# A hybrid encoder layer on one core: the forget gates' row and the first queries issued later, one chunk of values earlier

## The chip, the cores and the metric

The kernel runs on one core of one Trainium2 chip. The metric is the device time of one execution in microseconds; lower is better. The core has five engines that run side by side, each working off its own queue in order: TensorE (PE in the profile; its weight loads are PEld), VectorE (DVE), ScalarE (ACT), GpSimd (POOL), and SyncE (SP), which issues most of the DMA transfers. TensorE writes its results to PSUM, eight banks that VectorE and ScalarE read. Engines wait for each other only through semaphores: an instruction that waits holds up all that stand behind it in its own queue.

## The reference

One layer of a bidirectional encoder on 1024 tokens of width 1024, in float32. Cut to what matters:

```
mod = silu(c) @ w_ada + b_ada                      # six rows: shifts, scales, gates
h = modulate(rms_norm(x), sh1, sc1)
q_a, k_a, v_a, qk_m, v_m, o_m, gates = split(h @ w_in)
y_attn = attention(rope(norm(q_a)), rope(norm(k_a)), v_a)          # 8 heads of 64, 2 key heads
q, k = silu(conv5(qk_m))                                           # a 5-tap convolution along the tokens
i, f = gates (forward and backward); log_f = log_sigmoid(f)
h_fw, h_bw = mlstm(q, k, v_m, i, log_f), the same from the end     # 4 heads of 128
y_mem = norm(h_fw + h_bw) * sigmoid(o_m)
x = x + g1 * (concat(y_attn, y_mem) @ w_out)
x = x + g2 * ((silu(h2 @ w_gate) * (h2 @ w_up)) @ w_down),  h2 = modulate(rms_norm(x), sh2, sc2)
return rms_norm(x)
```

## The kernel before

**Products.** Each float32 product is made of three matmuls in a rounded format (`mm3`, L323 to L325): both operands are split into a high part (ScalarE, a copy: hh, whi) and the rest (VectorE or GpSimd, a subtraction: hl, wlo). Weights arrive by DMA as pieces (wst), are split into whi and wlo, and wait in a ring of six.

**A plan written as a program.** The order of all instructions is fixed before the run. The kernel's source steps through a clock of its own (`Clock`): chains of steps are put on a list of events with planned durations, and as the clock passes, each step issues its instruction. So each engine's queue holds its instructions in the order of planned times. The chip follows that order, but not the planned times: where it is later than planned on one engine, instructions behind the late one wait. `ck.chain(delay, step, step, ...)` starts after `delay` planned us; a Flag among the steps holds the chain until it is set; `LAT` = 0.14 lies between steps. A step that sets `ck.fin` lengthens itself to that time.

**Streams.** TensorE's work comes from generators. Main streams go first when they are ready, and fill streams take the rest (`streams`). The fill stream `un` works off the list `IN`, the units of the input projection:

- ("q", i): a pair of attention heads' queries;
- ("f", i): 128 channels of qk_m. `conv_unit` makes two halves of 512 tokens, 24 matmuls each into one PSUM tile acc; ScalarE evacuates each half to xp, and then VectorE runs five taps on all 1024 tokens (y), ScalarE a tanh, VectorE the last product, and SP stores y;
- ("t", i): 256 columns of v_m or o_m for all tokens, in eight blocks of 24 matmuls into acct; ScalarE evacuates each block to vstg and SP stores it. ("t", 1) is the second half of the values v_m, for the heads 2 and 3 of the memory; it needs four pieces of weights, a convolution unit two.

**The switch to attention.** `IN` first runs alone. When the last queries are rotated and stored (rope_ok[3]), the forget gates' logarithm is issued (logf_ok) and no sum is open in PSUM, the plan stops the stream between two halves or units (`ready`), closes the pool ps0 (six banks for acc and acct, two for the rest, among them ms) and opens ps1: one buffer for acc and acct together, two for T, two double ones for S, one for av. Then it calls `att_q(0)`, sets `attending`, and runs three main streams with `un` as fill: `scores` (S = queries times keys, VectorE's maximum sst, ScalarE's exp P, GpSimd's division), `turned` (transposes of P into T, split to PT by ScalarE and VectorE) and `values` (av). The first split of queries, `att_q(0)`, is a ScalarE copy to qs (high part) and a VectorE subtraction of its lower half; later heads have theirs on GpSimd.

**The gates.** `gate_steps` handles the 16 gate rows in two lists. The first ends with `logf`: VectorE writes the logarithm of the forget gates into T (T1 in the source). The second waits for logf_ok and `attending`; its first step `moved` is ScalarE's copy of that row to Fr. Then follow a mask (GpSimd), four scans, and the ends and rows (VectorE), exponentials (ScalarE), transposes and the last factors. `run(steps, apart, ...)` paces a list: `paced` sets `ck.fin = max(ck.fin, ck.now + apart)` after each step, and the second list has `apart` = PACE = 10.0, so its steps lie at least 10 planned us apart. Its end, gates_ok, is needed after attention only.

At the switch, ScalarE's queue thus has, in this order: the copy to Fr, the copy to qs, and the evacuation of the half that ended at the switch (the first half of ("f", 4)). Most instructions are issued by a helper, L102; they are told apart by their tiles.

Of the kernel before, what the change touches and what calls it, by code (L numbers as in the profile page):

```python
# [14 lines left out]
AF = mybir.ActivationFunctionType  # L15
# [31 lines left out]
AHEAD = 2  # L47
NP = NF // 2
IN = [("q", 2), ("q", 3), ("f", 0), ("f", 4), ("t", 2), ("f", 1),
      ("f", 5), ("f", 2), ("f", 6), ("t", 1), ("f", 3), ("f", 7), ("t", 3)]  # L50
MIX = [("o", i) for i in range(16)] + [("m", (i + 8) % 16) for i in range(16)]
FF = [("b", p) for p in range(NB)] + [("v", 0)] + [("s", (p, i)) for p in range(1, NP - 1) for i in range(2)] + [("v", NP - 1)]
SET = ["A11", "A12", "S2", "S3", "S1", "A22", "S4"]
# [77 lines left out]
class Clock:  # L131
# [12 lines left out]
    def run(self, eng, cost, two=False):  # L144
        s = max(self.free[eng], self.now)
        if two and self.lock and eng in self.two:
            other = "gps" if eng == "dve" else "dve"
            s = max([s] + [b for a, b in self.two[other] if a <= s < b])
            self.two[eng] = self.two[eng][-7:] + [(s, s + cost)]
        e = self.free[eng] = s + cost  # L150
        self.fin = max(self.fin, e)
# [109 lines left out]
def layer_kernel(ctx, tc, xT, c, w_ada, vecs, cons, rope, w_f, w_fT, w_t0, w_t, w_o, w_gu, w_d, out):  # L261
# [65 lines left out]
    def dma(dst, src, q=None):  # L327
        (q or nc.sync).dma_start(dst, src)
        on_chip = dst.space == src.space == bass.MemoryType.SB if hasattr(src, "space") else False
        return ck.dma(math.prod(dst.shape) * 4, 0.65 if on_chip else 0.5)  # L330
# [4 lines left out]
    ck = Clock()  # L335
    dve, act, gps = Engine(ck, nc.vector, "dve"), Engine(ck, nc.scalar, "act"), Engine(ck, nc.gpsimd, "gps")
# [11 lines left out]
    class slot:  # L348
# [11 lines left out]
        t = property(lambda self: self.flag().t)  # L360
# [15 lines left out]
    with tc.manual_schedule():  # L376
# [148 lines left out]
        def row_tile(name, tag="raw"):  # L525
            return gtp.tile([P, S], F32, tag=tag, name=name, bufs={"raw": 3, "row": 1}[tag])
# [434 lines left out]
        gates_ok, logf_ok, attending = Flag(), Flag(), Flag()  # L961
# [34 lines left out]
        def gate_steps():  # L996
# [17 lines left out]
            def soft(i):  # L1014
                if i == 0:
                    G["t"] = stp.tile([P, S], F32, tag="x", name="gt", bufs=KT)[64:P]
                    act.activation(G["t"], G["T1"][64:P], AF.Abs)
                elif i == 1:
                    act.activation(G["t"], G["t"], AF.Exp, scale=-1.0)
                else:  # L1020
                    act.activation(G["t"], G["t"], AF.Ln, bias=1.0)
# [15 lines left out]
            def scan(i):  # L1037
                F, I, mk = G["F"], G["T1"][0:64], G["mk"]
                if i == 0:
                    G["T2"] = row_tile("T2")  # L1040
                    M = G["M"] = G["T2"][0:64]
                    dve.tensor_tensor_scan(M[0:32], F[0:32], I[0:32], 0.0, op0=OP.add, op1=OP.max)
                elif i == 1:
                    dve.tensor_tensor_scan(G["M"][32:64, ::-1], F[32:64, ::-1], I[32:64, ::-1], 0.0,
                                                 op0=OP.add, op1=OP.max)
                elif i == 2:
                    B = G["B"] = F
                    dve.tensor_tensor_scan(B[0:32], mk[0:32], F[0:32], 0.0, op0=OP.mult, op1=OP.add)
                else:
                    dve.tensor_tensor_scan(G["B"][32:64, ::-1], mk[32:64, ::-1], F[32:64, ::-1], 0.0,  # L1050
                                                 op0=OP.mult, op1=OP.add)
# [24 lines left out]
            def exps(i):  # L1076
                if i == 0:
                    each(G["T1"][64:P], G["B"], mprev)
                elif i == 1:
                    act.activation(G["M"], G["M"], AF.Exp, scale=-1.0)  # L1080
                elif i == 2:
                    each(G["T2"][64:P], G["T1"][0:64], rend)
                else:
                    dve.tensor_add(rend, rend, mprev)
                    act.activation(rend, rend, AF.Exp)
# [43 lines left out]
            def run(steps, apart, flag, *before):  # L1129

                def paced(fn):
                    def go():
                        fn()
                        ck.fin = max(ck.fin, ck.now + apart)
                    return go

                out = [(None, f) for f in before]
                for e, f in steps:
                    out.append((e, (f[0], paced(f[1])) if isinstance(f, tuple) else paced(f)))
                ck.chain(0.5, *[f for _, f in out], (lambda: None), bg=[e for e, _ in out] + [None], flag=flag)  # L1140

            run([("gps", spaces), ("dve", spaced), (None, (slot("T"), lambda: rows(0))), (None, (slot("T"), lambda: rows(1))),
                 *[("act", lambda i=i: soft(i)) for i in range(3)], ("dve", logf)], 0.0, logf_ok)
            run([("act", moved), ("gps", mask), *[("dve", lambda i=i: scan(i)) for i in range(4)], ("dve", ends), ("dve", rows_r),
                 ("dve", rows_hl), *[("act", lambda i=i: exps(i)) for i in range(4)],
                 *[(None, (slot("T"), lambda i=i, b=b: columns(i, b))) for i in range(2) for b in range(2)],
                 ("dve", lambda: dve.tensor_scalar(cols[:, :, 1], cols[:, :, 1], QK, None, op0=OP.mult)),
# [24 lines left out]
        Q, Pt, PT = {}, {}, {}  # L1172
# [5 lines left out]
        def att_q(h):  # L1178
            if h:
                qd = ap.tile([P, S], F32, tag="qd", name="qd", bufs=1)  # L1180
                src = q_d[h // 2][(h % 2) * DH:(h % 2 + 1) * DH]
                dma(qd[0:DH], src)
                there = ck.chain(dma(qd[DH:P], src), lambda: None)
            else:
                qd, there = q0_at
            qs = ap.tile([P, S], F32R, tag="qs", name="qs")
            Q[h] = qs, ck.chain(0.0, there, *([] if h else [logf_ok]), lambda: act.activation(qs, qd, AF.Copy),
                                lambda: (gps if h else dve).tensor_sub(qs[DH:P], qd[DH:P], qs[DH:P].bitcast(F32)))

        def scores():  # L1190

            for q in range(NQ):
                h, j = divmod(q, NJ)
                if j == 2 and h + 1 < AH:
                    att_q(h + 1)
                ada_late()
                g, (qs, ok) = h // 4, Q[h]
                yield [ok, k2_ok[g]] + [slot("S")] + Tem[max(q - 3, 0):max(q - 2, 0)]
                sp, f = psum_tile([P, S], "S")
                for n in range(NH):  # L1200
                    for m in range(2):
                        nc.tensor.matmul(sp[:, halves(n)], qs[:, j * P:(j + 1) * P], k2[g][m][:, halves(n)],  # L1202
                                         start=m == 0, stop=m == 1)
                ck.pe(0.87)
                st = ap.tile([P, 4], F32, tag="sst", name="sst", bufs=8)
                cq = colq[:, j, h:h + 1]

                def top(st=st, sp=sp, cq=cq):
                    dve.reduce_max(st[:, 0:1], sp, axis=AX.X)
                    dve.tensor_scalar(st[:, 1:2], st[:, 0:1], cq, -1.0, op0=OP.mult, op1=OP.mult)  # L1210

                def exp(st=st, sp=sp, cq=cq, q=q, f=f):
                    Pt[q] = ap.tile([P, S], F32, tag="P", name="P", bufs=3)
                    act.activation(Pt[q], sp, AF.Exp, bias=st[:, 1:2], scale=cq, accum_out=st[:, 2:3])
                    f.set(ck, ck.fin + LAT)

                def norm(st=st, q=q):
                    gps.tensor_scalar(Pt[q], Pt[q], st[:, 3:4], 0.0, op0=OP.mult, op1=OP.add)

                ck.chain(LAT, top, exp, lambda st=st: dve.reciprocal(st[:, 3:4], st[:, 2:3]), norm, flag=Pok[q])  # L1220
# [968 lines left out]
        for n in range(NH):  # L2189
            def chunk_step(j, k):  # L2190
                ck.need(h_ok[n][k])
                if k == 0:
                    ck.need(slot("acct").flag())
                    tiles.append(psum_tile([P, 272], "acct"))
                s = slice(j * P, (j + 1) * P)
                mm3(tiles[j][0], (h_hi[k][:, s], h_lo[k][:, s]), weights(start["t", 0], k, 2), k == 0, k == KT - 1)
                ck.pe(0.38)
                if k == KT - 1:
                    chunk_out(0, j, *tiles[j])

            js = range(4 * n, 4 * n + 4)
            for k in range(KT - 2):
                for j in js:
                    chunk_step(j, k)
                if k % 2 and (n or k < 4):
                    load_piece()
            for j in js:
                for k in range(KT - 2, KT):
                    chunk_step(j, k)
            if n:  # L2210
                load_piece()
            if n == 0:
                while not again:
                    ck.pop()
                shift_sums()
            else:
                ck.chain(0.0, *vo_ok[0], gate_steps)
# [175 lines left out]
```

## Time and profile before

| | us |
|---|---|
| median of 3 runs | 1325.08 |
| lowest and highest run | 1324.16, 1325.69 |
| the profiled execution | 1330.26 |
| its span, first to last instruction | 1328.5 |
| mean granted TensorE clock | 0.989 |

| engine | busy us | share of the span |
|---|---|---|
| TensorE | 1272.7 | 96% |
| VectorE | 1047.4 | 79% |
| ScalarE | 701.3 | 53% |
| GpSimd | 508.4 | 38% |

The profile records one execution. Times in its rows are us from the first instruction; a row names engine, line, operation, and tiles as out<-in. Idle time before an instruction stands in brackets with the instruction that ended it. Busy shares are means over stages with different limits, so a stage is read by its own rows. The input projection alone runs until 144 us, attention with the units of `IN` beside it until about 481 us; ("t", 2) is the first chunk in it (163 to 233 us), ("t", 1) runs from 346 to 411 us, and ("t", 3) is the last unit.

### The profile page before, as it was taken

How to read it: one execution, taken by the hardware profiler on the slowest of the kernel's cores; microseconds unless marked ns; L12 is line 12 of the kernel's file. 1: busy time of each engine (PE TensorE's matmuls, PEld its weight loads, DVE VectorE, ACT ScalarE, POOL GpSimd, SP SyncE). 2: the span in 40 equal slices, each digit the busy share in tenths (PEclk: the TensorE clock that was granted, in tenths of full speed). 3: DMA queues.
4: the chain of work that ended last, by engine and by line, in shares of the span. 5: the costliest groups of instructions: out<-in, count | busy, mean ns of one | idle time of the engine just before them, and what ended most of it. 6: DMA issues, size and time to landing. Idle time of an engine off the chain costs nothing.

```text
span 1328.5 us, 19724 instructions
## 1 busy us (share of the span) xinstructions
PE 1272.7 (96%) x6656; PEld 1074.3 (81%) x6656; DVE 1047.4 (79%) x1701; ACT 701.3 (53%) x1327; POOL 508.4 (38%) x444
## 2 busy tenths in 40 slices
PE   9999799999999999999999999999999999999997
PEld 7887588788888888787877888888888887788886
DVE  7958798889867865999789988866776755888886
ACT  6583667687767645555586333233323334454453
POOL 0072376676755415432143255555545430000002
PEclk9999899999999999999999999999999999999999
DMA  9557433333323027633552443333333258833325
GB/s 374 186 151 195 130 114 118 102 99 110 119 91 102 25 98 250 217 109 112 188 183 80 141 146 134 107 115 112 103 103 119 72 184 319 311 97 96 95 59 164
DMA packets 104469, 187.04 MB, mean 141 GB/s; under 512 B 11568, under 2 KB 33200, under 8 KB 104368
## 3 DMA queue, kind: packets, MB, share of 16 engines
q1 hardware_dynamic: 91120, 163.81, 38.8%
q10 hardware_dynamic: 13248, 21.97, 4.4%
q8 instruction: 53, 0.87, 0.3%
q14 instruction: 48, 0.39, 0.1%
HBM read 139.33 MB, written 42.73 MB: 137 GB/s over the span
## 4 chain that ended last, share of the span: by engine, by line
PE 64%; DVE 15%; issue 8%; ACT 4%; DMA 4%; POOL 4%; SPq 1%; ACTq 0%; DVEq 0%; POOLq 0%
PE acc L325 17%; PE acc L323 17%; PE acc L324 16%; PE av L1255 2%; PE T L1234 2%; DVE sst L102 2%; DVE y L102 2%; DVE x L102 2%; PE S L1202 2%; DVE PT L102 2%; POOL hl L102 1%; POOL wlo L102 1%; PE acct L323 1%; PE U L1962 1%; PE acct L325 1%
## 5 line engine op out<-in xcount | busy, mean ns | idle before, releaser
L102 ACT ACTIVATE whi<-wst 128x512 fp32r<-128x512 f32 (+2 forms) x223 | 134.0, 606 | 142.1 <-PE acc L325 59.9
L102 POOL TENSOR_TENSOR wlo<-wst,whi 128x512 fp32r<-128x512 f32 x80 | 121.0, 1519 | 177.7 <-ACT whi L102 126.9
L324 PE MATMUL acc<-x,whi 128*128 128x512 f32 x352 | 137.1, 389 | 0.0
L102 DVE TENSOR_TENSOR wlo<-wst,whi 128x512 fp32r<-128x512 f32 (+2 forms) x143 | 94.6, 666 | 34.6 <-ACT whi L102 34.2
L102 POOL TENSOR_SCALAR P<-P,sst 128x1024 f32<-128x1024 f32 x64 | 84.6, 1325 | 76.3 <-DVE sst L102 61.4
L323 PE MATMUL acc<-hh,whi 128*128 128x512 f32 x224 | 97.0, 433 | 9.9 <-ACT xp L102 8.7
L102 POOL TENSOR_TENSOR wlo<-wr,whi 128x512 fp32r<-128x512 f32 x52 | 72.6, 1395 | 72.1 <-ACT whi L102 68.2
L102 DVE TENSOR_TENSOR PT<-T,PT 128x512 fp32r<-128x512 f32 x128 | 84.1, 682 | 20.0 <-ACT PT L102 20.0
L102 POOL TENSOR_TENSOR x<-x,ny 128x256 f32<-128x256 f32 (+1 forms) x8 | 8.3, 1068 | 234.7 <-PE acc L325 214.8
L323 PE MATMUL acc<-whi,wch 128*128 128x512 f32 x244 | 95.7, 392 | 2.5 <-ACT wch L102 2.5
L325 PE MATMUL acc<-whi,wcl 128*128 128x512 f32 x244 | 96.1, 394 | 1.6 <-DVE wcl L102 1.6
L324 PE MATMUL acc<-wlo,wch 128*128 128x512 f32 x244 | 95.6, 392 | 0.0
L102 ACT ACTIVATE PT<-T 128x512 fp32r<-128x512 f32 x128 | 72.9, 596 | 31.6 <-PE T L1234 30.4
L324 PE MATMUL acc<-hl,whi 128*128 128x512 f32 x224 | 88.8, 397 | 0.3 <-DVE hl L102 0.3
L325 PE MATMUL acc<-hh,wlo 128*128 128x512 f32 x224 | 88.9, 397 | 0.1
L102 ACT ACTIVATE P<-S,sst,colq 128x1024 f32<-128x1024 f32 x64 | 77.2, 1206 | 21.5 <-DVE sst L102 20.5
L102 ACT ACTIVATE whi<-wr 128x512 fp32r<-128x512 f32 x56 | 35.4, 632 | 100.5 <-DVE wr L102 48.4
L323 PE MATMUL acct<-whi,hh 128*128 128x256 f32 (+1 forms) x256 | 79.1, 309 | 8.0 <-ACT vstg L102 5.8
L1234 PE MATMUL T<-ident,P 128*128 128x128 f32 x512 | 73.4, 276 | 8.3 <-DVE PT L102 6.5
L102 DVE TENSOR_REDUCE sst<-S 128x1 f32<-128x1024 f32 x64 | 77.7, 1214 | 4.4 <-PE S L1202 3.4
L324 PEld LDWEIGHTS acc<-x,whi 128*128 128x128 f32 x352 | 66.1, 188 | 13.8
L325 PE MATMUL acct<-whi,hl 128*128 128x256 f32 (+1 forms) x256 | 74.1, 289 | 1.9 <-POOL hl L102 1.9
(483 smaller groups left out, 3827.7 us busy)
## 6 DMA issues: line engine op xcount, KB each, us to landing
wr<-in_w_gu_dram SPq DMA_DIRECT2D x66, 256.0 KB, 2.7
ada<-in_w_ada_dram SPq DMA_DIRECT2D x64, 256.0 KB, 3.0
wd<-in_w_d_dram SPq DMA_DIRECT2D x22, 512.0 KB, 6.6
wst<-in_w_gu_dram SPq DMA_DIRECT2D x42, 256.0 KB, 2.9
wst<-act_d SPq DMA_DIRECT2D x33, 256.0 KB, 3.8
ada<-in_w_ada_dram SPq DMA_DIRECT2D x16, 512.0 KB, 7.7
wst<-in_w_o_dram SPq DMA_DIRECT2D x32, 256.0 KB, 3.6
act_d<-sg ACTq DMA_DIRECT2D x29, 256.0 KB, 2.0
```

Of the source, the lines that this page charges most:

```text
L102: return fn(*args, **kw)
L323: nc.tensor.matmul(acc, w[0], x[0], start=first, stop=False)
L324: nc.tensor.matmul(acc, w[0], x[1], start=False, stop=False)
L325: nc.tensor.matmul(acc, w[1], x[0], start=False, stop=last)
L1202: nc.tensor.matmul(sp[:, halves(n)], qs[:, j * P:(j + 1) * P], k2[g][m][:, halves(n)], start=m == 0, stop=m == 1)
L1234: nc.tensor.transpose(tp[:, k], Pt[q][:, (4 * b + k) * P:(4 * b + k + 1) * P], ident)
L1255: nc.tensor.matmul(av, va[:, k, h // 4], PT[it, b][m][:, k - 4 * b], start=(k, m) == (0, 0), stop=(k, m) == (NJ - 1, 1))
L1962: nc.tensor.matmul(U, T[:, i], wv[:, i], start=True, stop=True)
```

## The change

Three edits.

1. The second list of the gates gets a new first step `wait`, which issues nothing and sets `ck.fin` to 6.0 us later. It is paced like the other steps of the list.
2. The chain of `att_q(0)` starts 3.0 planned us after the call instead of at once; the later heads keep 0.0.
3. In `IN`, ("t", 1) moves from behind ("f", 6) to behind ("f", 1), so ahead of ("f", 5), ("f", 2) and ("f", 6).

```diff
 IN = [("q", 2), ("q", 3), ("f", 0), ("f", 4), ("t", 2), ("f", 1),
-      ("f", 5), ("f", 2), ("f", 6), ("t", 1), ("f", 3), ("f", 7), ("t", 3)]
+      ("t", 1), ("f", 5), ("f", 2), ("f", 6), ("f", 3), ("f", 7), ("t", 3)]
...
-            run([("act", moved), ("gps", mask), *[("dve", lambda i=i: scan(i)) for i in range(4)], ("dve", ends), ("dve", rows_r),
+            def wait():
+                ck.fin = ck.now + 6.0
+
+            run([(None, wait), ("act", moved), ("gps", mask), *[("dve", lambda i=i: scan(i)) for i in range(4)], ("dve", ends), ("dve", rows_r),
...
-            Q[h] = qs, ck.chain(0.0, there, *([] if h else [logf_ok]), lambda: act.activation(qs, qd, AF.Copy),
+            Q[h] = qs, ck.chain(0.0 if h else 3.0, there, *([] if h else [logf_ok]), lambda: act.activation(qs, qd, AF.Copy),
                                 lambda: (gps if h else dve).tensor_sub(qs[DH:P], qd[DH:P], qs[DH:P].bitcast(F32)))
```

The instructions are the same in kind and number; what changes is their order in each engine's queue. As the order follows from planned times, the later order can differ in other places too.

## The prediction, made before the changed kernel ran

> **What bounds the kernel now.** I read the page first, then TensorE's waits in the stretch where attention runs (140 to 500 us), then the timelines of TensorE, ScalarE and VectorE around the one large hole, then the clock in short windows.
>
> The page's busy shares, and TensorE's own waits (who waited for whom, total us, times, longest):
>
> ```profile
> PE 1272.7 (96%) x6656; PEld 1074.3 (81%) x6656; DVE 1047.4 (79%) x1701; ACT 701.3 (53%) x1327; POOL 508.4 (38%) x444
> ...
> PE acc L323 <- ACT xp L102: 8.7, 3, 7.0
> ```
>
> TensorE is busy 96% of the span, so over long distances the end moves by what TensorE idles or loses in clock. One wait of 7.0 us stands out: a matmul into acc waits for ScalarE's evacuation of an earlier acc into xp. TensorE's timeline there (start, duration, in brackets the idle time before and its releaser):
>
> ```profile
> 143.64 0.39 PE L325 MATMUL acc<-hh,wlo 128*128 128x512 f32 x1
> 151.01 0.79 PE L323 MATMUL acc<-hh,whi 128*128 128x512 f32 x1 [6.98 <-ACT xp L102]
> ...
> 158.48 1.98 PE L1202 MATMUL S<-k,qs 128*128 128x512 f32 x8
> ...
> 163.27 0.53 PE L323 MATMUL acct<-whi,hh 128*128 128x256 f32 x1 [2.14 <-ACT xp L102]
> ```
>
> At 143.64 + 0.39 = 144.03 the first half of unit ("f", 4) ends. There the plan opens the PSUM pool ps1, and the second half waits until 151.01. ScalarE's queue at that time, complete from 144 to 163 us:
>
> ```profile
> 144.13 0.58 ACT L102 ACTIVATE xp<-acc 128x512 f32<-128x512 f32 x1
> 148.34 1.05 ACT L102 ACTIVATE Fr<-T 64x1024 f32<-64x1024 f32 x1 [3.62 <-DVE T L102]
> 149.41 1.06 ACT L102 ACTIVATE qs<-qd 128x1024 fp32r<-128x1024 f32 x1
> 150.38 0.58 ACT L102 ACTIVATE xp<-acc 128x512 f32<-128x512 f32 x1
> 156.11 0.63 ACT L102 ACTIVATE whi<-wst 128x512 fp32r<-128x512 f32 x1 [5.15 <-PE acc L324]
> 159.86 1.28 ACT L102 ACT_TABLE_LOAD   x1 [3.13 <-DVE y L102]
> 161.16 1.06 ACT L102 ACTIVATE xp<-y 128x1024 f32<-128x1024 f32 x1
> 162.12 0.61 ACT L102 ACTIVATE whi<-wst 128x512 fp32r<-128x512 f32 x1
> 162.64 0.58 ACT L102 ACTIVATE xp<-acc 128x512 f32<-128x512 f32 x1
> ```
>
> The xp row at 144.13 evacuates unit ("f", 0). Then the queue stands still for 3.62 us, because Fr (the forget gates' row) needs VectorE's T; qs (the first head's queries) follows, and only then comes the evacuation at 150.38, which had been possible since 144.7. Why T is late, VectorE's queue shows:
>
> ```profile
> 146.13 2.17 DVE L102 SCALAR_TENSOR_TENSOR T<-T,gt 64x1024 f32<-64x1024 f32 x1
> 148.33 1.23 DVE L102 TENSOR_TENSOR qg<-qg,sw 128x1024 f32<-128x1024 f32 x1
> 149.47 0.16 DVE L102 SCALAR_TENSOR_TENSOR rqv<-rqv,ms 128x16 f32<-128x16 f32 x1
> 149.56 0.81 DVE L102 TENSOR_SCALAR y<-xp,vec 128x1024 f32<-128x1024 f32 x1
> ...
> 151.58 3.99 DVE L102 SCALAR_TENSOR_TENSOR y<-xp,vec,y 128x1024 f32<-128x1024 f32 x3
> 155.61 1.22 DVE L102 TENSOR_TENSOR qs<-qd,qs 64x1024 fp32r<-64x1024 f32 x1
> ...
> 157.47 2.31 DVE L102 SCALAR_TENSOR_TENSOR y<-xp,vec,y 128x1024 f32<-128x1024 f32 x1
> 159.71 1.21 DVE L102 TENSOR_REDUCE sst<-S 128x1 f32<-128x1024 f32 x1
> ...
> 167.45 1.23 DVE L102 TENSOR_REDUCE sst<-S 128x1 f32<-128x1024 f32 x1 [1.23 <-PE S L1202]
> ```
>
> VectorE has no pause here but the one of 1.23 us at 167.45. So beside TensorE there is a second limit of nearly the same length: what VectorE must work off in order. TensorE's holes also cost clock (windows; the figure after the POOL column is the granted clock, 1.00 is full):
>
> ```profile
> 151.00:156.30 5.30, 5.29 (x13) 4.13 (x14) 5.13 (x8) 0.19 (x1) 0.00 (x0) 0.50 0.83 247
> 163.20:167.20 4.00, 3.93 (x16) 3.70 (x17) 3.02 (x4) 3.33 (x6) 3.82 (x5) 0.57 0.26 101
> 550.50:554.50 4.00, 3.81 (x25) 3.21 (x26) 3.90 (x10) 3.17 (x9) 1.61 (x1) 1.00 0.76 219
> ```
>
> The first two windows follow the holes of 6.98 and 2.14 us, the third this one:
>
> ```profile
> 550.62 0.63 PE L2110 MATMUL tr<-ident,hs 128*128 128x128 f32 x4 [2.00 <-DVE W L102]
> ```
>
> After the first two the clock is about half for 4 to 5 us; after 2.00 us it stays full. I take it that a hole under 2 us costs no clock.
>
> **The evacuation goes first.** In the new order Fr and qs come after the evacuation on ScalarE. It can start when the 144.13 row ends, at 144.71, and ends 0.58 later, at 145.29. By that alone the second half would start at 145.3, 5.7 us sooner. But the plan opens a new pool at this point, and a pool's memory is handed over as a whole: the first matmul in ps1 waits for the last reader of every tile of ps0. In the kernel's program it carries two waits, one for ScalarE's evacuation and one for VectorE's rqv<-rqv,ms, which reads the old pool's ms. In the trace that one ends at 149.47 + 0.16 = 149.63; now it is hidden behind the evacuation's end, 150.96, and afterwards it is late next. What runs ahead of rqv on VectorE is issued before the pool opens and isn't touched. With the 0.05 us that lie between 150.96 and 151.01, the restart moves to 149.68: **1.33 us** sooner. The hole is still 5.65 us, so I leave the half clock behind it as it is.
>
> The Trainium skill, "TensorE: Matmul & The Clock Gate", section "Part 1: The HAM clock gate", says that the clock falls to half after an idle window of about 3.4 us. By that a hole of 5.65 us costs clock as one of 6.98 does, and the trace agrees at 0.50; the 0.57 after only 2.14 us is earlier than the page's rule has it. By the page alone the term of 1.7 us below would be nothing, and the sum 1.7 us smaller.
>
> **The second half.** From 151.01 its first 21 matmuls take until 158.48, and three more end the half at 0.2 each (half of 5.30 us / 13, the window at clock 0.50): 8.1 us to the last start, so from 149.68 it ends near 158.0. In between, the first scores S stood at 158.48. They need the queries' split, which the plan now starts 3.0 us after the switch instead of at once; the half itself is planned at 8 steps of 0.65 = 5.2 us. On ScalarE qs now stands behind the whi row (156.11, which came 5.10 us after the restart): 149.68 + 5.10 + 0.6 = 155.4, and with 1.06 us it ends at 156.5, no longer waiting for anything else (T ends at 148.3). On VectorE the subtraction of 1.22 us falls behind the fifth tap, which stood after it. Three taps end at 155.57; what lies between 156.83 and 157.47 (an ada piece, 0.64) and a tap of 1.33 (a third of 3.99) to 2.31 lead to 157.6 or 158.6, the subtraction to 158.8 or 159.8. I take 159.3. TensorE thus waits **1.3 us** for the queries, a cost, but a hole under 2 us. S of two blocks then takes 1.98 us as in its row, to 161.3.
>
> **The next unit.** The chunk behind it (acct, 163.27) shares the single acc buffer and waits for the second half's evacuation, which stays behind the tanh of ("f", 0). That needs the fifth tap, now at about 158.1 instead of 159.78: table load 1.28, tanh 1.06, whi 0.5 and evacuation 0.58 lead to 161.5, so the chunk starts at 161.55 instead of 163.27. Its hole shrinks from 2.14 to about 0.3 us, a gain of **1.7 us**, and with it goes the half clock after it: 4.0 us at 0.57 is a loss of 4.0 x 0.43 = **1.7 us**.
>
> Sum on TensorE, at the third block of scores: -1.33 + 1.3 - 1.7 - 1.7 = **-3.4 us**.
>
> **What VectorE allows.** The first step of the forget gates' list on VectorE is a scan:
>
> ```profile
> 181.08 2.26 DVE L102 TENSOR_TENSOR_SCAN T<-Fr,T 32x1024 f32<-32x1024 f32 x1
> ```
>
> The first reduction moves from 159.71 to some 160.3 (+0.6), the pause of 1.23 at 167.45 goes, so there VectorE is only 0.6 sooner. The list's wait step is paced like every step of that list, so it holds that list back by PACE = 10 planned us, not by 6.0. Each step of it takes the place of the next one, and the scan of 2.26 us at 181.08 leaves the stretch in which VectorE is full. That makes -0.6 - 2.26 = **-2.9 us**. The two limits agree within half a us; I take their middle, -3.1. The delayed list has one step more at its end, near 270 us; I cost it at nothing, as the moved chunk lies there.
>
> **The moved chunk.** ("t", 1) goes ahead of ("f", 5), ("f", 2) and ("f", 6): the same matmuls, four weight pieces ahead of six, eight v_d stores sooner on SP's queue and the three convolutions' stores later. Both kinds are read only after attention, which covers them. VectorE's load in the two kinds of unit:
>
> ```profile
> 260.00:280.00 20.00, 18.21 (x105) 15.04 (x103) 18.69 (x25) 16.12 (x36) 16.31 (x12) 1.00 0.20 67
> 380.00:400.00 20.00, 19.04 (x144) 17.73 (x143) 10.35 (x23) 12.31 (x26) 9.10 (x8) 1.00 0.30 90
> ```
>
> A chunk asks little of VectorE (10.35 of 20 us, against 18.69 under convolutions). Having it sooner eases a loaded stretch and then puts five convolutions in a row. TensorE idles 1.8 us in the first window and 1.0 in the second, so the swap can be worth a few us either way. I count it at nothing, and keep 3 us to both sides.
>
> Altogether -3.1 us on a span of 1328.5. The profiled execution took 1330.26, 5.2 us over the median of 1325.08; the difference carries over to the median: **1322.0 us**.
>
> **Rivals.** *VectorE takes it all back.* Only the first 1.33 us is won and later reductions and PT subtractions eat the rest: 1325.1 - 1.3 = 1323.8, down to nothing. For it: VectorE's full queue. Against: the scan leaves it. That is also the case in which the change hardly does what it says, as the pool's handover keeps TensorE waiting anyway.
>
> *The chunk's own hole goes too.* In its old place the chunk has this one:
>
> ```profile
> 367.17 0.38 PE L323 MATMUL acct<-whi,hh 128*128 128x256 f32 x1 [2.07 <-ACT vstg L102]
> ```
>
> Its evacuation stood behind a pooled ada step on ScalarE. In a new place the queue is different, and 2.07 us plus a similar loss of clock, about 4 us with it, may vanish: 1322.0 - 4 = 1318.0. Against it: another such hole may open.
>
> *Slower: the gates' tail lands on the path.* VectorE's steps of that list after the scans:
>
> ```profile
> 230.49 2.05 DVE L102 COPY mprev<-T 32x7 f32<-32x7 f32 x2
> 232.55 1.22 DVE L102 TENSOR_TENSOR T<-T,Fr 64x1024 f32<-64x1024 f32 x1
> ```
>
> Ten us later these and the ones behind them meet the taps of ("f", 1), in the window where VectorE is at 18.69 of 20. If two such pairs (6.5 us) make the transposes wait for PT in full, the time is 1322.0 + 6.5 = 1328.5. It decides once these waits exceed the 3.1 us won.
>
> **How the numbers follow.** Chances: forecast 0.45, VectorE takes it back 0.25, chunk's hole goes 0.15, slower 0.15. I set 0.2% (2.65 us) as what a measurement of this kernel tells from no change. The forecast lies just beyond it; its own range is 1320 to 1324, and I put 0.3 of its 0.45 beyond. Faster: 0.3 + 0.15 = 0.45; the same: 0.15 + 0.25 = 0.40; slower: 0.15. The range runs from 1317.5 (chunk's hole gone) to 1326.5 (the swap's 3 us on the wrong side of the second case).
>
> **What would show it.** Right: a hole of about 5.6 us, ended by VectorE's rqv and not by xp; first S near 159; the chunk at 161 to 162 at full clock; scans some 10 us later against the units. Wrong: a restart near 145.3 (the pool does not hold it, and some 4 us more are won, if VectorE lets them), half clock at the chunk, or new holes over 2 us between 200 and 480.

## The result, and the profile after

| | before | after |
|---|---|---|
| median, us (7 runs each) | 1326.02 | 1319.64 |
| lowest and highest | 1324.16, 1328.34 | 1316.42, 1322.17 |
| ratio, 95% interval | | 0.9955 [0.9944, 0.9965] |
| profiled execution | 1330.26 | 1319.32 |
| its span | 1328.5 | 1317.5 |

The change makes the kernel 0.45% faster, 6.4 us. The two profiled executions differ by 10.9 us, because the one of before lies 4.2 us over its median; a difference between the two traces is read with that in mind.

The page of the changed kernel, first part:

```profile
PE 1268.9 (96%) x6656; PEld 1073.3 (81%) x6656; DVE 1050.5 (80%) x1711; ACT 695.9 (53%) x1317; POOL 503.7 (38%) x439
```

TensorE's matmuls are the same 6656. The other engines' instructions are not quite the same in kind and number, though the description of the change says so: five pieces of the product `ada` are now made by VectorE (41, were 36) instead of GpSimd and ScalarE (39, were 44), because the plan gives some of these pieces to VectorE when that is free in planned time. That by itself is not the gain: the kernel e3 below has the same 41 and 39 and is slower. TensorE's busy time falls by 3.8 us (mean granted clock 0.991, was 0.989) and the span by 11.0. TensorE's timeline at the switch:

```profile
148.55 0.77 PE L323 MATMUL acc<-hh,whi 128*128 128x512 f32 x1 [4.47 <-DVE rqv L102]
...
157.53 0.39 PE L323 MATMUL acct<-whi,hh 128*128 128x256 f32 x1 [0.98 <-ACT xp L102]
...
159.54 3.20 PE L1205 MATMUL S<-k,qs 128*128 128x512 f32 x8 [1.03 <-DVE qs L102]
```

ScalarE's queue there, complete from 142.8 to 162 us:

```profile
142.86 0.58 ACT L102 ACTIVATE xp<-acc 128x512 f32<-128x512 f32 x1
144.11 0.60 ACT L102 ACTIVATE xp<-acc 128x512 f32<-128x512 f32 x1 [0.67 <-PE acc L325]
153.66 0.63 ACT L102 ACTIVATE whi<-wst 128x512 fp32r<-128x512 f32 x1 [8.95 <-PE acc L324]
154.19 1.04 ACT L102 ACTIVATE qs<-qd 128x1024 fp32r<-128x1024 f32 x1
156.37 0.63 ACT L102 ACTIVATE whi<-wst 128x512 fp32r<-128x512 f32 x1 [1.13 <-PE acc L324]
156.90 0.58 ACT L102 ACTIVATE xp<-acc 128x512 f32<-128x512 f32 x1
157.50 1.28 ACT L102 ACT_TABLE_LOAD   x1
158.79 1.06 ACT L102 ACTIVATE xp<-y 128x1024 f32<-128x1024 f32 x1
```

and VectorE's rows that decide there, with one of GpSimd that ran beside the last:

```profile
148.24 0.17 DVE L102 SCALAR_TENSOR_TENSOR rqv<-rqv,ms 128x16 f32<-128x16 f32 x1
...
157.13 1.28 POOL L102 TENSOR_TENSOR wlo<-wst,whi 128x512 fp32r<-128x512 f32 x1 [1.03 <-ACT whi L102]
157.21 2.28 DVE L102 TENSOR_TENSOR qs<-qd,qs 64x1024 fp32r<-64x1024 f32 x1
```

The half at the switch is now evacuated at once (144.11), yet the unit's second half starts only when rqv, the last reader of the old PSUM pool, is done. The second half too is now evacuated ahead of the tanh (156.90, then the table load), so the chunk behind it starts at 157.53, where it stood at 163.27. The first S comes at 159.54, where it stood at 158.48: all five taps are done before the queries' subtraction.

Where the time went, by windows (after the length: busy us of TensorE, its weight loads, VectorE, ScalarE, GpSimd; then the granted clock). The second window ends where the memory's first products of queries and keys start (tr<-mq,mk). Before, then after:

```profile
144.00:250.00 106.00, 89.34 (x575) 79.25 (x575) 96.39 (x141) 68.11 (x129) 63.98 (x47) 0.94 0.38 114
250.00:501.22 251.22, 239.51 (x1558) 210.61 (x1557) 195.51 (x327) 175.55 (x348) 136.20 (x116) 0.99 0.31 94
```

```profile
144.00:250.00 106.00, 94.62 (x613) 84.50 (x613) 94.28 (x143) 71.75 (x138) 69.13 (x49) 0.95 0.39 115
250.00:490.59 240.59, 230.05 (x1521) 204.09 (x1520) 197.41 (x335) 165.62 (x326) 125.77 (x107) 1.00 0.31 97
```

The stage from the switch to the memory takes 346.6 instead of 357.2 us, with 2132 matmul records in both; from there to the end both take 827 us. TensorE idles 106 - 89.34 = 16.7 us in the first window before and 11.4 after, 11.7 and 10.5 in the second. Of the 10.6 us, 5.3 are idle time ahead of 250 us, 1.2 idle time behind it, and 4.2 a shorter busy time for the same work. Only half of the 5.3 lies at the switch: up to 165 us TensorE idles 6.5 instead of 9.1 us, from 200 to 250 us 2.3 instead of 5.0.

### The profile page after: what moved, and what is told of

Its sections match the earlier page's. It is cut to its first block, busy times and chain, and to the rows that moved or that the text cites. A ratio compares the mean times of both kernels' runs of the same rounds, so it can differ in the third digit from the quotient of the medians.

```text
span 1317.5 us, 19699 instructions
## 1 busy us (share of the span) xinstructions
PE 1268.9 (96%) x6656; PEld 1073.3 (81%) x6656; DVE 1050.5 (80%) x1711; ACT 695.9 (53%) x1317; POOL 503.7 (38%) x439
## 4 chain that ended last, share of the span: by engine, by line
PE 67%; DVE 15%; issue 7%; ACT 5%; DMA 4%; POOL 1%; SPq 0%; ACTq 0%; DVEq 0%; POOLq 0%
PE acc L325 17%; PE acc L323 17%; PE acc L324 17%; PE av L1258 3%; PE T L1237 3%; PE S L1205 3%; DVE x L102 2%; DVE sst L102 2%; DVE y L102 1%; DVE PT L102 1%; PE acct L323 1%; PE acct L325 1%; PE acct L324 1%; PE ni L2049 1%; PE U L1965 1%
## 5 line engine op out<-in xcount | busy, mean ns | idle before, releaser
L323 PE MATMUL acc<-hh,whi 128*128 128x512 f32 x224 | 96.4, 430 | 7.1 <-DVE rqv L102 4.5
L323 PE MATMUL acc<-whi,wch 128*128 128x512 f32 x244 | 95.8, 393 | 2.2 <-ACT wch L102 2.2
L323 PE MATMUL acct<-whi,hh 128*128 128x256 f32 (+1 forms) x256 | 77.8, 304 | 6.0 <-ACT vstg L102 5.0
```

Source lines behind the costliest of these rows:

```text
L323: nc.tensor.matmul(acc, w[0], x[0], start=first, stop=False)
```

## The experiments

**1. The three edits one by one, and the first two together** (each against the kernel before). The diffs are those of the change, cut to the edit: e1 has the wait step alone, e2 the 3.0 of att_q(0) alone, e3 the order of units alone, e4 edits 1 and 2:

```diff
-      ("f", 5), ("f", 2), ("f", 6), ("t", 1), ("f", 3), ("f", 7), ("t", 3)]
+      ("t", 1), ("f", 5), ("f", 2), ("f", 6), ("f", 3), ("f", 7), ("t", 3)]
```

is e3, for instance.

> Edit 1 alone: the gates' list waits, the queries' split stays at the switch. ScalarE's order is then qs, evacuation of the first half of (f, 4). qs still waits for the old tiles that VectorE's T (ends near 148.3) reads, so the evacuation ends near 150.0 and TensorE restarts there instead of 151.0. Theory 'switch' (the gain comes from what stands ahead of the evacuation and behind it): little at the hole, 1 us, and up to 2.3 us from the scan that leaves the full stretch of VectorE: ratio 0.9975 to 0.9992. Theory 'chunk' (the gain comes from the earlier chunk of values): no change, 0.999 to 1.001.

> Edit 2 alone: the queries' split 3 planned us later, the gates' list at the switch. ScalarE's order is Fr, evacuation, whi, qs, whi, evacuation of the second half, tanh. Fr waits for T, so the evacuation ends near 150.0 and TensorE restarts 1 us sooner; but the second half's evacuation is ahead of the tanh, so the chunk behind it starts some 3 us sooner. Theory 'switch': ratio 0.997 to 0.999. Theory 'chunk': 0.999 to 1.001.

> Edit 3 alone: (t, 1) ahead of three convolutions. All queues are as in the kernel before until the second half of (f, 1), near 245 us; the hole of 7 us stays. Theory 'switch': no more than the new order's accidents, 0.998 to 1.002. Theory 'chunk': most of the gain, 0.995 to 0.997.

> Edits 1 and 2 without 3. All queues are as in the changed kernel until the end of (f, 1), near 250 us. Theory 'switch': most of the gain, 0.9955 to 0.9975. Theory 'chunk': 0.999 to 1.000; a third, that the gain is an accident of the new order as a whole, would show as a sum of the parts that is far from the whole.

Measured: e1 0.9975 [0.9958, 0.9993], e2 1.0077 [1.0054, 1.0099], e3 1.0071 [1.0043, 1.0099], e4 1.0081 [1.0058, 1.0104]. Alone, two of the three edits cost 0.7 to 0.8%, and the first two together cost 0.8%; all three win 0.45%. The parts do not add. e1 lies at the edge of what 'switch' said of it, but e2, e3 and e4 lie outside both theories, so neither the switch nor the chunk holds the gain by itself. e4 is the sharper case: every queue of it is that of the changed kernel until some 250 us, the switch included, and it ends 18 us later (1337.8 against 1319.6).

What e4 has in common with the changed kernel is its lead by then. TensorE from 144 to 250 us in e1, e2 and e4:

```profile
144.00:250.00 106.00, 89.70 (x594) 79.80 (x595) 95.74 (x144) 68.25 (x128) 66.77 (x47) 0.97 0.35 107
144.00:250.00 106.00, 91.62 (x565) 80.56 (x565) 88.82 (x132) 64.84 (x126) 66.98 (x46) 0.92 0.33 104
144.00:250.00 106.00, 92.97 (x607) 83.19 (x608) 94.56 (x141) 71.15 (x139) 70.70 (x50) 0.95 0.36 115
```

Before, 575 matmuls ran in that time, in the changed kernel 613. With edit 1 alone they are 594, with edit 2 alone 565, with both 607. So by this count, in which matmuls differ in size, the full lead ahead of 250 us comes with edits 1 and 2 together and with neither alone. The third edit, which acts later, decides whether the lead is kept.

**2. The switch by itself.** Three kernels keep a planned order and change only the switch. e5 is the changed kernel with the new PSUM pool handed over tile by tile:

```diff
-        PP["pool"] = tc.tile_pool(name=name, bufs=bufs, space=PSUM)
+        PP["pool"] = tc.tile_pool(name=name, bufs=bufs, space=PSUM, reuse_waits="tile" if name == "ps1" else "pool")
```

> The changed kernel with one difference: the PSUM pool opened at the switch takes over its banks tile by tile, not as a whole, so its first matmul waits for nothing. The order in all queues is that of the changed kernel. All theories: the restart moves from 148.6 to about 144.1 us, the second half ends near 149.5, its hole and half clock go. Theory 'TensorE counts' (a hole filled on TensorE is time won): 4.5 us of hole and 2.4 us of clock are won, about 7 us, a ratio to the kernel before of 0.990. Theory 'VectorE holds the scores': the first S waits for the queries' subtraction, which stands behind five taps on VectorE, and those start no sooner; the idle time only moves to the place ahead of S, S stays at 159.5 within 0.5 us and the ratio stays that of the changed kernel, 0.994 to 0.997.

e8 is the kernel before with the copies to Fr and qs put behind the first evacuation in ScalarE's queue, while the planned clock counts them where they were (cut to one of the two copies):

```diff
-                act.activation(G["F"], G["T1"][64:P], AF.Copy)
+                later(act, G["F"], G["T1"][64:P], AF.Copy)
...
+def later(eng, *args):
+    n = max(math.prod(a.shape[1:]) for a in args if hasattr(a, "shape"))
+    eng.clock.run(eng.name, eng.cost("activation", n, args, {}))
+    HELD.append(lambda: eng.eng.activation(*args))
```

> The kernel before with its planned order untouched, but the copies to Fr and qs issued on ScalarE right behind the first half's evacuation. That is the switch as the change has it, without any other difference in order. Theory 'the site': the restart is at 149.7, ended by VectorE's rqv; S and all behind it come 1.3 us sooner, ratio 0.998 to 0.999. Theory 'order of the whole plan': what the change wins does not come from here, ratio 0.999 to 1.001, and no marker behind 250 us is more than 2 us from the kernel before.

e9 is its mirror: the changed kernel, its clock untouched, with both copies issued ahead of the first evacuation (cut in the same way):

```diff
+            if not h:
+                EARLY[0]()
+                nc.scalar.activation(qs, qd, AF.Copy)
```

> The changed kernel with its order untouched, but the copies to Fr and qs really issued on ScalarE ahead of the first half's evacuation, as in the kernel before. Theory 'the site': the restart goes back by some 1.3 to 2.4 us (to about 150.5, ended by xp), and with it all of the time that the change won at the switch: ratio to the kernel before 0.9975 to 0.999. Theory 'order of the whole plan': the first S waits for the subtraction either way, and the ratio stays at 0.994 to 0.997.

Measured: e5 0.9959 [0.9946, 0.9973], e8 1.0002 [0.9986, 1.0017], e9 0.9953 [0.9937, 0.9970]. TensorE's timeline in e5, where S stands:

```profile
159.32 3.78 PE L1205 MATMUL S<-k,qs 128*128 128x512 f32 x8 [8.17 <-DVE qs L102]
```

in e8:

```profile
151.39 0.76 PE L332 MATMUL acc<-hh,whi 128*128 128x512 f32 x1 [7.31 <-DVE rqv L111]
159.47 2.11 PE L1213 MATMUL S<-k,qs 128*128 128x512 f32 x8 [1.40 <-DVE qs L111]
164.83 0.38 PE L332 MATMUL acct<-whi,hh 128*128 128x256 f32 x1 [2.58 <-ACT xp L111]
```

and in e9:

```profile
149.99 0.80 PE L328 MATMUL acc<-hh,whi 128*128 128x512 f32 x1 [6.57 <-ACT xp L107]
159.16 0.39 PE L328 MATMUL acct<-whi,hh 128*128 128x256 f32 x1 [0.98 <-ACT xp L107]
159.97 2.00 PE L1220 MATMUL S<-k,qs 128*128 128x512 f32 x8
```

In e5 the hole of 4.47 us is gone from its place and stands, with more, ahead of S: S comes at 159.32, where it came at 159.54. Idle time on TensorE won ahead of S is not time won; VectorE's subtraction holds S. In e8 rqv ends the wait, as the pool demands, and the time is that of before. (Its memory starts at 499.13, 2.1 us from the 501.22 of before, where at most 2 was expected.) But in its profiled execution ScalarE and VectorE were 1.6 us late ahead of the switch already, so the restart, at 151.39, is no sooner than before; and 1.3 us, 0.1%, lies within its interval. e8 alone does not settle what an earlier restart is worth. In e9 the hole is back, ended by xp, and the full gain is kept. So where the first half's evacuation stands, and the hole behind it, are worth nothing that these runs can tell: e5 rules out the 7 us of its first theory, and an effect of 1 to 2 us lies within the intervals, but in e5 the place of S shows that the hole was not won. What e9 keeps and e8 lacks is the planned order: among it the second half's evacuation ahead of the tanh, which lets the chunk start at 159.16, not 164.83.

**3. Is it the fill's last unit?** In e4 four whole blocks of ("t", 3) stand ahead of attention's end, in the changed kernel not one whole block. e10 is e4 with that unit held back:

```diff
             for kind, i in order:
+                if (kind, i) == ("t", 3):
+                    yield [att_done]
```

> Edits 1 and 2 without the moved chunk (that was 1337.8 us), and the last unit of the fill stream, ('t', 3), held back until attention's main streams are done, so that none of its blocks stands among them. Theory 'displaced': the four blocks (about 11.6 us of TensorE) that stood ahead of attention's end pushed attention back, and the memory's stage has room for them: attention ends near 490 instead of 501 us, ratio to the kernel before 0.998 to 1.001. Theory 'starved': once the convolutions are used up, attention is held by its own chain (scores, maximum, exponential, division, transposes), the blocks only filled its idle time: attention still ends near 500 us, TensorE's holes grow instead, and the time is no better than 1337, ratio 1.007 to 1.016.

Measured: 1.0191 [1.0175, 1.0206], slower than either theory said. The last group of av matmuls starts at 501.31, in e4 at 500.54: attention ends no sooner without the blocks. TensorE's windows, e4 and then e10:

```profile
455.00:511.00 56.00, 52.47 (x404) 49.59 (x404) 40.13 (x67) 32.80 (x63) 16.75 (x18) 1.00 0.20 57
```

```profile
455.00:511.00 56.00, 43.14 (x271) 38.27 (x271) 38.95 (x66) 29.94 (x54) 13.77 (x17) 0.88 0.12 36
```

Without the blocks TensorE idles 12.9 of 56 us instead of 3.5, at a lower clock. The theory 'displaced' fell: the blocks filled time in which attention had nothing ready. Attention was late already when it came there, and the question is where it lost its lead.

**4. Pairs of edits, and the chunk the other way.** Adding the parts forbids what the planned order foretells for two pairs. e11 has edits 1 and 3, e12 edits 2 and 3. e13 and e14 move ("t", 1) to the other side, e13 with edit 1:

```diff
-      ("f", 5), ("f", 2), ("f", 6), ("t", 1), ("f", 3), ("f", 7), ("t", 3)]
+      ("f", 5), ("f", 2), ("f", 6), ("f", 3), ("f", 7), ("t", 1), ("t", 3)]
```

> Edits 1 and 3 together, without 2. Theory 'parts add': edit 1 alone gave -0.25%, edit 3 alone +0.7%, so about +0.46%, a ratio of 1.003 to 1.006. Theory 'planned order': the parts act only through the order that the kernel's own planned clock works out, in which the end of attention's main streams stands against the start of the fill stream's last unit, ('t', 3). The planned end of this variant is 19.3 us behind that of the kernel before (the four variants with losses so far had planned ends 5.5 to 20.8 us behind it, and lost 10 to 25 us), with attention's mains ending 27 planned us later: ratio 1.010 to 1.018, attention's last av near 510 us, and four or more blocks of ('t', 3) ahead of it.

> Edits 2 and 3 together, without 1. Theory 'parts add': edit 2 alone gave +0.77%, edit 3 alone +0.71%, so about +1.5%, a ratio of 1.012 to 1.018. Theory 'planned order': the planned end is 3.7 us behind that of the kernel before, mains 10 planned us later: ratio 1.000 to 1.007, and faster than e2 and e3, each of which it contains.

> Edit 1, and ('t', 1) moved the other way: behind ('f', 7), so two units later than in the kernel before. Theory 'chunk sooner eases VectorE': this is the wrong way, six convolutions stand in a row beside attention, and it is slower than edit 1 alone by some us: ratio 1.000 to 1.006. Theory 'planned order': planned end 2.7 us ahead of the kernel before, the earliest of the orders looked at: ratio 0.993 to 0.999.

> Only the order of units: ('t', 1) behind ('f', 7), nothing else changed. Theory 'chunk sooner eases VectorE': slower than the kernel before, ratio 1.002 to 1.008. Theory 'planned order': planned end 1.4 us ahead of the kernel before, mains ending 1 planned us sooner: ratio 0.995 to 1.000.

Measured: e11 1.0211 [1.0193, 1.0229] with the last group of av at 509.26; e12 1.0056 [1.0043, 1.0069]; e13 1.0005 [0.9995, 1.0016]; e14 1.0009 [0.9996, 1.0022]. e11 is 28 us slower, where adding said 6; e12 loses about a third of what adding said (1.5%), and is no slower than either of its parts; that it is faster than they are, the intervals do not show. The planned order had the sign and the size of both, a little short for e11. For e13 and e14 it had gains of some us and there are none: a few us it does not tell. Nor does it tell the gain of the change, whose planned end is 0.9 us behind that of before. That the earlier chunk eases VectorE is left open: e13 lies in the range of that theory and is slower than e1, e14's ratio lies below its range.

**Where attention loses its lead.** In most of the slow kernels VectorE stands still for the gates' transposes (T<-ident,T, the steps `columns` of the second list). Who waited for whom on VectorE, 150 to 505 us, in e4 and in e11 (total us, times, longest):

```profile
DVE cols L102 <- PE T L1091: 7.1, 1, 7.1
```

```profile
DVE cols L102 <- PE T L1091: 13.1, 2, 7.6
```

These four steps share the two T buffers of PSUM with attention's transposes of P. How much of attention's transposing gets through in the 40 us from the first of them on, the windows of that one line show (TensorE's busy us and matmuls first). In the order before, after, e4, e11:

```profile
312.60:352.60 40.00, 9.87 (x68) 7.77 (x68) 1.00 0.36 106
```

```profile
322.35:362.35 40.00, 8.24 (x59) 6.89 (x60) 1.00 0.33 100
```

```profile
330.90:370.90 40.00, 4.63 (x32) 3.72 (x32) 1.00 0.29 96
```

```profile
335.94:375.94 40.00, 2.43 (x16) 1.82 (x16) 0.96 0.27 90
```

In e11 attention runs at a quarter of its pace there, and TensorE's queue holds fill blocks in its place: 8 matmuls of S in 40 us, 32 before, but 42 of the fill stream's L323, 23 before. Why the plan does that is in the source:

```python
                def take():
                    dve.tensor_copy(cols[:, 4 * b:4 * b + 4, 2 * qi:2 * qi + 2],
                    ...
                    f.set(ck, ck.fin + LAT)

                ck.at(0.6, take)
                ck.fin = ck.now + 0.9
```

`f` marks the T buffer as free. `take` runs 0.6 planned us behind its step and reads `ck.fin`, which only a step of a chain sets back to the present. If no chain's step falls into these 0.6 us, `ck.fin` still holds the end of the paced step, PACE = 10 later, and the plan counts the buffer as taken for 10.1 us, not for about 1.5. In e11, for one, the step at planned 295.57 frees its buffer at 305.71. Attention's transposes then have one buffer in the plan, and fill blocks are ordered ahead of them; on the chip the buffer is free, but the order stands. Whether that happens to a step depends on what else falls into 0.6 planned us:

| kernel | edits | planned end against before, us | steps that keep T for 10 planned us | attention's transposes in 40 us | VectorE's wait for the gates' T, us | ratio |
|---|---|---|---|---|---|---|
| before | | 0 | 0 | 68 | none listed | 1 |
| e14 | chunk late | -1.4 | 0 | 64 | none listed | 1.0009 |
| e13 | 1, chunk late | -2.7 | 0 | 62 | 0.8 | 1.0005 |
| e1 | 1 | +0.4 | 0 | 58 | 0.2 | 0.9975 |
| after | 1, 2, 3 | +0.9 | 1 | 59 | 1.8 | 0.9955 |
| e12 | 2, 3 | +3.7 | 1 | 52 | 8.6 | 1.0056 |
| e2 | 2 | +5.5 | 1 | 48 | 0.7 | 1.0077 |
| e3 | 3 | +11.7 | 2 | 48 | 5.7 | 1.0071 |
| e4 | 1, 2 | +11.7 | 3 | 32 | 7.1 | 1.0081 |
| e11 | 1, 3 | +19.3 | 4 | 16 | 13.1 | 1.0211 |

The third and fourth columns are the source's own planning, no measurement. The wait in the sixth does not go with the loss (e2 0.7 us at 1.0077, e12 8.6 at 1.0056), the transposes in the fifth go with it better. No kernel without such a step is more than 0.1% slower than before; every kernel with one is 0.6 to 2.1% slower, except the changed kernel, whose one step falls where attention keeps its pace. This account fits the ten orders, but stands on the source and on a comparison of kernels that differ in much else: it is argued, not shown by a run of its own. A kernel in which `take` sets `ck.fin` back first would test it; none was run, nor was the changed kernel with that mended. Worked out again with that one line, the plan alone has attention end 31.9 planned us sooner in e11 and 20.0 in e4, and the same as it was in the kernel before; so the stale value does reach the plan, but what it costs on the chip is not measured. Nor is it all that e4 loses: from 280 to 300 us, ahead of the first of these transposes at 330.90, TensorE is busy 16.05 us at a granted clock of 0.83, in the changed kernel 19.18 at 1.00. A hole of 3.38 us stands there in e4, ended by an evacuation to xp at 291.15.

Why the changed kernel is 6.4 us faster than the kernel before, neither of which loses attention's pace, is settled only in part. The lead ahead of 250 us is there in full wherever edits 1 and 2 are both in (607 matmuls in e4, 610 in e5, 613 after, 620 in e9) and nowhere else (575 before, 569 in e8, 565 in e2, 594 in e1), with the hole at the switch or without it. So it lies in the order, not in the hole. Which step of that order gives it stays open.

## Why the prediction was right, and where it was not

The time is right, and in part by luck: 1322.0 was said for a kernel of 1325.1, a gain of 3.1 us. The gain is 6.4, twice that. 1319.6 lies inside the range of 1317.5 to 1326.5 and on the side of "faster", but just below the 1320 to 1324 that the prediction gave its main case. The first two edits, which were to win the 3.1 us, lose 10.7 by themselves, and the moved chunk, which was put at nothing, wins some 17 in their company; that the two end near the forecast was not foreseen. The reasons hold in part.

- **The pool's handover**: right. The hole is ended by rqv, not xp; it is 4.47 us, not 5.65, because VectorE was 1.2 us sooner in that execution (rqv at 148.24, was 149.47). The half clock stayed. But the term of -1.33 us, counted as won, is not seen: e5 removes the whole hole and S comes no more than 0.2 us sooner, and e9 puts it back and loses nothing. That the restart carries the end with it failed, as what follows waits for VectorE.
- **S waits for the queries**: right in place (159.54 for "159.3"), by two differences that cancel. VectorE's taps were 1.2 us sooner, and the subtraction took 2.28 us where 1.22 stood in its row of before.
- **"I take it that a hole under 2 us costs no clock"**: fell. Behind the holes of 0.98 and 1.03 us S ran at a mean granted clock of 0.62 and took 3.20 us for 1.98.
- **The second half's evacuation "stays behind the tanh"**: fell, in the kernel's favour: it came ahead, and the chunk started at 157.53, not 161.55.
- **The sum on TensorE, -3.4**: up to 165 us TensorE idles 2.6 us less in the profiled pair, which is near it. But e5 idles 9.2 us there, as the kernel before did (9.1), and is as fast as the changed kernel, so idle time up to 165 us is no measure of the gain. What is kept is the work done by 250 us; the pair of e8 and e9 differs by 6.5 us of idle time up to there (18.1 and 11.6 of 106). That the chunk no longer waits may be part of it; by itself it was not tried.
- **What VectorE allows, -2.9**: the first scan came at 188.83, 7.8 us later where 10 were said. e1, which moves it too (to 195.6), is 3.3 us faster, by its interval 0.9 to 5.6. That fits the term; in other company (e4, e11) it does not come out as time.
- **"The delayed list ... I cost it at nothing"** and the moved chunk, **"I count it at nothing, and keep 3 us to both sides"**: here the prediction is wrong by size. By the ratios, the first two edits lose 10.7 us without the moved chunk and win 6 with it: the chunk is worth some 17 us in that company and costs 9.4 alone. The bounds of 3 us came from VectorE's load in two windows. What counts, as argued above, is which of the gates' four transposes keep a buffer in the plan. The prediction saw the tail of that list only as VectorE's work, not as TensorE's and PSUM's.
- **The rivals**: "VectorE takes it all back" is wrong for the whole, though right for the hole itself (e5). "The chunk's own hole goes too" came about, and its 1318.0 is nearer to the result than the forecast's 1322.0: from 170 to 480 us no hole of the changed kernel is over 1.3 us. But the kernel of e8, which has before's order, shows that hole at 1.73 us and full clock and is no faster, so the 3 us beyond the forecast can't be put there with any certainty. "The gates' tail on the path" is what e4 and e11 show, by another way than VectorE's steps.

## What to carry to other kernels

Where a program works out its order from planned times, an edit is not one place: compare the orders from the edit to the end, and look for the stage in which the main work loses its pace, before the place of the edit is priced. Run the parts and the pairs; when they do not add, the sum of the parts explains nothing. And a hole is worth filling only as far as what stands behind it is ready: ask what the instruction after next waits for.

## What the runs showed of the hardware that was not expected

TensorE's clock does not go by the length of the last hole alone. Single holes of 2.07 and 2.14 us before, 2.21 in e11 and 2.58 in e8 left a granted clock of 0.57 to 0.64 in the 4 us behind them; one of 2.76 us in e1, which ended at 162.33, left 1.00. In the changed kernel S ran at 0.62 (3.20 us for eight matmuls) behind holes of 0.98 and 1.03 us that lay 1 us apart. It ran at full clock behind 1.40 us in e8 (2.11 us) and, with 0.98 us ahead of the chunk, in e9 (2.00 us). The Trainium skill, "TensorE: Matmul & The Clock Gate", section "A second HAM failure mode: psum-queue depth-cycling", says that frequent short pauses between groups of matmuls can make the clock swing between half and full. The rows of S in the changed kernel fit that; those of e8 and e9 show that one such pause need not. The idle window of about 3.4 us that the prediction cites from that page covers neither the lower clock behind 2.07 us nor this one.

VectorE's subtraction of the queries (64x1024) took 1.22 us in eight of the runs and 2.19 to 2.28 us in the other six (the changed kernel, e4, e8, e9, e10, e12). In these six GpSimd had begun a subtraction of weights (wlo<-wst,whi) before it and ran beside it, in the changed kernel from 157.13 to 158.41; in the eight it had not. So the 1.22 us that the prediction took from its row holds only where GpSimd has not begun such a step.
